# One weight array in order of use, two constant loads, tanh merge gates, new numbers in the order model, and two key tiles transposed back to back in a decoder block's attention

## The chip, the cores and the metric

The kernel runs on one core of a Trainium2 chip. The metric is the device time of one execution in microseconds (us). TensorE (PE in the profile) multiplies matrices and transposes, and a weight load (PEld) goes with each of its instructions. VectorE (DVE), ScalarE (ACT) and GpSimd (POOL) work element by element. SyncE (SP) issues the transfers (DMAs) in the kernel before.

## The reference, cut to what matters

```python
h = rms_norm(x, norm_pre); proj = h @ w_in            # x: 512 x 1024, w_in: 1024 x 6936, float32
q_n,k_c,v_c,k_s,v_s,k_w,v_w,g_n,z_n,q_r,k_r,v_r,z_r,m_a,m_b = split(proj)
# mixer A: sparse attention, 8 heads of 64 in 2 groups, causal: compressed, selected and window branch
o_a = g0 * attend(q_n, kc, vc) + g1 * attend(q_n, k_s, v_s) + g2 * attend(q_n, k_w, v_w)
#   kc, vc = gelu((16-strided blocks of 32 keys + position table) @ w1) @ w2
y_a = (o_a * silu(z_n)) @ w_nsa_o
# mixer B: retention, 4 heads, chunks of 128 rows, group norm
y_b = (retention(rot(q_r), rot(k_r), v_r) * silu(z_r)) @ w_ret_o
merged = sigmoid(m_a) * y_a + sigmoid(m_b) * y_b
y = x + rms_norm(merged @ w_out, norm_post)
```

## The kernel before

**Arithmetic.** To keep float32 precision, each operand of a product is split into a high part `hi` (rounded to the format `FR` that TensorE takes at full rate) and a low part `lo = x - hi`. Each product is three matmuls (`mm3`: hi·hi, hi·lo, lo·hi), 128 rows by 512 columns for most. For each half of a weight block ScalarE (seldom VectorE) makes `whi<-raw`, and VectorE or GpSimd makes `wlo<-raw,whi` (`split_lo`, with `sub_split`). `either` picks GpSimd where the order model says that it would be done sooner.

**Stages on TensorE, in order.** Block A (the first 512 columns: keys and values; eight steps `k`, all four row tiles in each), block C (280 columns: more keys and values, the branch gates), Q, the two hidden layers of the compressed keys (`hidden`), and then the blocks of `PLAN`: Z, MA, ZR, QK, VR and so on, last the output projection. The work of attention and of retention stands between these matmuls. Around block A stands the start: the input arrives transposed in eight tiles (`load_xT`), is scaled by `gp` and split (`hTh`, `hTl`); `WAKE` matmuls on an identity matrix run before it.

**Attention.** `att_head` makes a score tile (L840 is its masked minimum, then `exp` on ScalarE, a reciprocal and a scaling on VectorE). `att_block` transposes the probabilities of four heads for one key tile into one PSUM bank (four float32 transposes, L220), ScalarE and VectorE split them, and two matmuls add their product with the values to `po`. Two banks, the ring `PT`, serve all transposes.

**Transfers.** A load takes 1024 columns of weights (512 KB) into one of four `raw` buffers; `load_next` issues it once the load four before it is split. All are issued from SP's queue in program order. The loads cut their rows out of the weight arrays as these are given, in runs of 1 or 2 KB; some need two DMAs. `const_loads` issues ten small DMAs: rotary table, position tables (four), gate bias, `w2` (four). `positions` brings the position tables into their layout with two transposes on TensorE, in the middle of block A.

**What sets the order.** Nothing is scheduled on the chip: every engine takes its instructions in the order written. The class `Order` walks through coroutines, one for each piece of work, and issues the one that its own clock says is ready (`od.pe`, `od.op`, `od.dma` add costs and hold each engine's time). `LAG` and `PE_LAG` are the delays that it allows between an engine's result and its use. An operation that in truth comes later than the model says makes its user wait on the chip.

**Gates.** `tail_m` makes `sgs = sigmoid(m * rsrow)` on ScalarE; `tail_ya` and `tail_yb` multiply it with `y_a` and `y_b`. The other functions in use at that time are `exp` and `tanh`.

Of the kernel before, what the change touches and what calls it, by code (L numbers as in the profile page):

```python
# [18 lines left out]
P = 128  # L19
# [12 lines left out]
LAG, PE_LAG = 150.0, 110.0  # L32
# [4 lines left out]
WAKE = 10  # L37
# [3 lines left out]
class Order:  # L41
# [5 lines left out]
    def __init__(self):  # L47
        self.now = 0.0
        self.eng = {"act": 0.0, "dve": 0.0, "pool": 0.0, "dma": 0.0}
        self.ring = 500.0  # L50
        self.port = 0.0
        self.cos, self.n = [], 0
        self.flags = set()
# [15 lines left out]
    def op(self, e, cost, r=0.0, port=False):  # L69

        self.eng[e] = self.begin(e, r, port) + cost + ISSUE
        if port:
            self.port = self.eng[e]
        return self.eng[e]

    def dma(self, nbytes, r=0.0, n=1):
        for _ in range(n):
            self.ring = max(self.ring, r + LAG) + 475
            self.eng["dma"] = max(self.eng["dma"], self.ring + 625) + nbytes / n / 360.0
        return self.eng["dma"] + 910 - LAG  # L80
# [31 lines left out]
class Ring:  # L112
# [11 lines left out]

    def put(self, x, r=0.0):
        self.free.append((r, x))
# [3 lines left out]
def block_kernel(ctx: ExitStack, tc, x, xT, g_pre, w_in, b_gate, pe_k, w1_k, w2_k,  # L130
                 pe_v, w1_v, w2_v, w_nsa_o, w_ret_o, w_out, norm_post,
                 rope_n, rope_r, dmask, out):
# [82 lines left out]
    def mm(ps, a, b, start, stop, r=0.0, cost=None):  # L215
        T.matmul(ps, a, b, start=start, stop=stop)  # L216
        return od.pe(cost or max(0.4435 * size(b) + 1, 107 if a.shape[-1] > 64 else 54), r)

    def tr(ps, a, idn, r=0.0):
        T.transpose(ps, a, idn)  # L220
        return od.pe(56 if a.dtype == FR else 109, r)
# [5 lines left out]

    def either(n, r):

        return "dve" if od.begin("dve", r, True) + 1.04 * n <= od.begin("pool", r, True) + 2.36 * n else "pool"  # L230
# [59 lines left out]
    loads = []  # L290

    def add_block(w, c0, n, nk, perm=False, single=0):
        for c in range(nk // 2):
            def ld(raw, c=c):
                if c < single:
                    for k in range(2):
                        r0 = c * 256 + k * P
                        DMA.dma_start(raw[:, k * n:(k + 1) * n], w[r0:r0 + P, c0:c0 + n])
                    return
                DMA.dma_start(raw[:, :2 * n].rearrange("p (k n) -> p k n", k=2),  # L300
                              w[c * 256:(c + 1) * 256, c0:c0 + n].rearrange("(k p) n -> p k n", p=P))
            loads.append((ld, 2 * n, 2 if c < single else 1, perm))

    def add_w1(w1):
        w1v = w1.rearrange("(h l d) n -> h d l n", h=2, l=16)
        for c in range(4):
            def ld(raw, c=c):
                for hf in range(2):
                    DMA.dma_start(raw[hf * 64:(hf + 1) * 64].rearrange("p (l n) -> p l n", l=4),
                                  w1v[hf][:, 4 * c:4 * c + 4, :])  # L310
            loads.append((ld, 1024, 2, False))

    def add_qk(hp):
        for c in range(4):
            def ld(raw, c=c):
                rv = raw.rearrange("p (k n) -> p k n", k=2)
                for i, c0 in enumerate((C_QR, C_KR)):
                    DMA.dma_start(rv[:, :, i * 256:(i + 1) * 256],
                                  w_in[c * 256:(c + 1) * 256, c0 + hp * 256:c0 + hp * 256 + 256]
                                  .rearrange("(k p) n -> p k n", p=P))  # L320
            loads.append((ld, 1024, 2, False))

    def add_nsa_o(half):
        for c in range(2):
            def ld(raw, c=c):
                rv = raw.rearrange("p (k n) -> p k n", k=2)
                for g in range(2):
                    DMA.dma_start(rv[g * 64:(g + 1) * 64],
                                  w_nsa_o[g * 256 + c * 128:g * 256 + (c + 1) * 128, half * 512:(half + 1) * 512]
                                  .rearrange("(k p) n -> p k n", p=64))  # L330
            loads.append((ld, 1024, 2, False))

    add_block(w_in, C_A, 512, KD, single=1)
    add_block(w_in, C_C, 280, KD)
    add_block(w_in, C_Q, 512, KD)
    add_w1(w1_k)
    add_w1(w1_v)
    for name, i in PLAN:
        if name == "Z":
            add_block(w_in, C_Z, 512, KD, True)  # L340
        elif name == "QK":
            add_qk(i)
        elif name == "NO":
            add_nsa_o(i)
        elif name == "RO":
            add_block(w_ret_o, i * 512, 512, KD)
        else:
            add_block(w_in, {"ZR": C_ZR, "VR": C_VR, "MA": C_MA, "MB": C_MB}[name] + i * 512, 512, KD)
    for half in range(2):
        add_block(w_out, half * 512, 512, KD)  # L350
# [8 lines left out]

    def load_next():  # L360
        i = len(raws)
        if i < len(loads):
            raw = rp.tile([P, 1024], FT, name="raw", tag="raw", bufs=NR)
            loads[i][0](raw)
            raws.append((raw, od.dma(P * loads[i][1] * 4, parts[2 * (i - NR) + 1][2] if i >= NR else 0.0, loads[i][2])))
# [9 lines left out]
    def splitter():  # L375
        for i, (_, n, _, perm) in enumerate(loads):
            for k in range(2):
# [17 lines left out]
                if perm:  # L395
                    src = src.rearrange("p (g j c) -> p g j c", g=2, j=4)
                    vh, vl = (v.rearrange("p (j g c) -> p g j c", g=2, j=4) for v in (vh, vl))
# [70 lines left out]
    gp = cp.tile([P, KD], FT, name="gp")  # L468
    ss = cp.tile([P, NT], FT, name="ss")
# [55 lines left out]
    ropen = cp.tile([P, NT, 32], FT, name="ropen")  # L525
    bg = cp.tile([P, 24], FT, name="bg")
# [3 lines left out]
    pes = [cp.tile([P, 16], FT, name=f"pe{i}") for i in range(2)]  # L530
    pen = [at(40 + 0.5 * i, P)[0:32] for i in range(2)]
# [46 lines left out]
    def vals(src, br, t, r):  # L578
        for g in range(2):
            sv = src[:, g * 64:(g + 1) * 64]  # L580
            e = act(VS[:, t, br, g, g, :], sv, r=r)
            e = sub_split(VS[:, t, br, g, 1 - g, :], sv, VS[:, t, br, g, g, :], e, either(64, e))
        return e

    def tail_a(t, ps, e, ring):
# [13 lines left out]
        yield od.need("pos")  # L599
# [261 lines left out]
    def att_block(t, g, br, b, kt, slots, lastblk):  # L861
# [3 lines left out]
        pt = yield from PT.get()  # L865
        for j in range(4):
            e = tr(pt[:, j * P:(j + 1) * P], slots[j]["pv"][:, b, kt * P:(kt + 1) * P], ident, r)
        if lastblk:
            for s in slots:
                PR.put(s["P"], e)  # L870
        phl = yield from PHL.get()
# [31 lines left out]
    def att_unit(t, g, brs, slots):  # L903
        yield lambda: all("r" in s for s in slots)
        todo = [(br, b, kt) for b, br in enumerate(brs) for kt in range(t + 1)]
        for i, (br, b, kt) in enumerate(todo):
            od.spawn(att_block(t, g, br, b, kt, slots, i == len(todo) - 1), 2)
# [9 lines left out]
    def att_sum(t, g, po):  # L917
# [12 lines left out]
        e = tt(gv, low[m].rearrange("p (j c) -> p j c", j=4), gv, OP.mult, e, either(512, e))  # L930
# [37 lines left out]
    def tail_qk(hp, t, ps, e):  # L968
# [17 lines left out]
        on = either(512, e)  # L986
# [420 lines left out]
```

## Time and profile before

| what | us |
|---|---|
| three runs: median, lowest, highest | 536.37, 535.72, 537.97 |
| the profiled execution: its time | 536.74 |
| its span in the trace | 534.8 |
| busy in the span: TensorE, weight loads | 521.1, 437.2 |
| busy in the span: VectorE, ScalarE, GpSimd | 387.9, 265.2, 36.5 |

The span is the part of an execution that the trace shows. The profiled execution took 1.9 us more than its span, and stands 0.37 us above the median. Busy times of different engines overlap. A matmul of 512 columns is written as 0.39 us long, but the next one starts 0.227 us after it: the records overlap, and a short wait hides in them.

### The profile page before, as it was taken

How to read it: one execution, taken by the hardware profiler on the slowest of the kernel's cores; microseconds unless marked ns; L12 is line 12 of the kernel's file. 1: busy time of each engine (PE TensorE's matmuls, PEld its weight loads, DVE VectorE, ACT ScalarE, POOL GpSimd, SP SyncE). 2: the span in 40 equal slices, each digit the busy share in tenths (PEclk: the TensorE clock that was granted, in tenths of full speed). 3: DMA queues.
4: the chain of work that ended last, by engine and by line, in shares of the span. 5: the costliest groups of instructions: out<-in, count | busy, mean ns of one | idle time of the engine just before them, and what ended most of it. 6: DMA issues, size and time to landing. Idle time of an engine off the chain costs nothing.

```text
span 534.8 us, 7434 instructions
## 1 busy us (share of the span) xinstructions
PE 521.1 (97%) x2642; PEld 437.2 (82%) x2642; DVE 387.9 (73%) x911; ACT 265.2 (50%) x560; POOL 36.5 (7%) x50
## 2 busy tenths in 40 slices
PE   8989998999999999999999999999999999999995
PEld 7778787888788887888888888888888888888885
DVE  6589889889698889999867877796746245346433
ACT  6562588456689576375645243553414234114411
POOL 1000020000004000030000120100000000000000
PEclk9999999999999999999999999999999999999999
DMA  8861137514014013251321424130825052404022
GB/s 313 295 215 56 43 80 235 159 30 110 21 39 119 1 34 100 65 158 41 96 82 43 135 63 134 40 120 13 301 79 144 14 157 84 146 8 157 2 88 108
DMA packets 34837, 55.22 MB, mean 103 GB/s; under 512 B 4336, under 2 KB 14448, under 8 KB 34800
## 3 DMA queue, kind: packets, MB, share of 16 engines
q1 hardware_dynamic: 34800, 54.75, 33.3%
q8 instruction: 20, 0.33, 0.2%
q14 instruction: 17, 0.14, 0.1%
HBM read 52.64 MB, written 2.10 MB: 102 GB/s over the span
## 4 chain that ended last, share of the span: by engine, by line
PE 78%; DVE 10%; DMA 5%; ACT 3%; issue 2%; SPq 1%; POOL 0%; POOLq 0%; DVEq 0%; ACTq 0%
PE bank L216 73%; PE bank L220 5%; DVE arena_f L195 3%; DVE wlo L195 2%; DMA arena_f<-in_x_dram 2%; DVE arena_r L195 1%; DMA arena_f<-in_xT_dram 1%; DMA raw<-in_w_in_dram 1%; ACT arena_f L183 1%; ACT L183 1%; ACT arena_r L183 1%; DMA raw<-in_cmp_w_v_dram 1%; DVE arena_f L204 1%; DVE arena_f L208 1%; DVE arena_f L840 1%
## 5 line engine op out<-in xcount | busy, mean ns | idle before, releaser
L183 ACT ACTIVATE whi<-raw 128x512 fp32r<-128x512 f32 x150 | 90.2, 626 | 55.9 <-PE bank L216 47.3
L195 DVE TENSOR_TENSOR wlo<-raw,whi 128x512 fp32r<-128x512 f32 x145 | 96.3, 699 | 12.3 <-ACT whi L183 10.4
L216 PE MATMUL bank<-whi,hTh 128*128 128x512 f32 x256 | 99.6, 404 | 0.1
L216 PE MATMUL bank<-wlo,hTh 128*128 128x512 f32 x256 | 96.6, 392 | 0.1
L216 PE MATMUL bank<-whi,hTl 128*128 128x512 f32 x256 | 96.3, 391 | 0.0
L216 PE MATMUL bank<-arena_r 128*128 128x256 f32 (+2 forms) x328 | 70.3, 335 | 0.6 <-DVE stat L840 0.4
L183 ACT ACTIVATE arena_r<-bank 128x512 fp32r<-128x512 f32 (+2 forms) x80 | 44.6, 570 | 39.6 <-PE bank L220 35.6
L216 PE MATMUL bank<-hTh,whi 128*128 128x512 f32 x160 | 63.7, 398 | 0.0
L216 PE MATMUL bank<-hTh,wlo 128*128 128x512 f32 x160 | 62.5, 391 | 0.0
L216 PE MATMUL bank<-hTl,whi 128*128 128x512 f32 x160 | 62.4, 390 | 0.0
L216 PE MATMUL bank<-arena_r,whi 128*128 128x512 f32 x192 | 59.1, 389 | 0.0
L216 PEld LDWEIGHTS bank<-arena_r 128*128 128x128 f32 x328 | 51.3, 189 | 7.8 <-DVE stat L840 0.9
L216 PEld LDWEIGHTS bank<-whi,hTl 128*128 128x128 f32 x256 | 48.0, 188 | 10.6
L216 PEld LDWEIGHTS bank<-wlo,hTh 128*128 128x128 f32 x256 | 48.1, 188 | 8.8 <-DVE wlo L195 0.8
L216 PEld LDWEIGHTS bank<-whi,hTh 128*128 128x128 f32 x256 | 48.0, 188 | 8.4 <-ACT whi L183 0.3
L195 DVE TENSOR_TENSOR arena_r<-bank,arena_r 128x512 fp32r<-128x512 f32 (+2 forms) x72 | 46.6, 655 | 9.3 <-ACT arena_r L183 8.7
L216 PE MATMUL bank<-whi,arena_r 128*128 128x512 f32 (+1 forms) x176 | 48.8, 352 | 0.0
L220 PE MATMUL bank<-ident,arena_f 128*128 128x128 f32 (+2 forms) x262 | 39.4, 274 | 4.6 <-DVE arena_f L560 2.6
L220 PEld LDWEIGHTS bank<-ident,arena_f 128*128 128x128 f32 (+2 forms) x262 | 31.2, 139 | 13.6 <-DVE arena_f L560 3.3
L216 PEld LDWEIGHTS bank<-arena_r,whi 128*128 128x128 f32 x192 | 36.0, 188 | 7.5
L216 PE MATMUL bank<-arena_r,wlo 128*128 128x512 f32 x96 | 37.3, 389 | 0.0
L183 ACT ACTIVATE arena_f<-arena_f,stat 128x512 f32<-128x512 f32 (+3 forms) x64 | 35.3, 555 | 2.2 <-DVE stat L840 2.1
(124 smaller groups left out, 708.7 us busy)
## 6 DMA issues: line engine op xcount, KB each, us to landing
raw<-in_w_in_dram SPq DMA_DIRECT2D x43, 512.0 KB, 4.5
raw<-in_w_in_dram SPq DMA_DIRECT2D x18, 256.0 KB, 3.1
arena_f<-in_x_dram SPq DMA_DIRECT2D x8, 512.0 KB, 6.3
raw<-in_w_ret_o_dram SPq DMA_DIRECT2D x8, 512.0 KB, 4.8
raw<-in_w_out_dram SPq DMA_DIRECT2D x8, 512.0 KB, 4.3
arena_f<-in_xT_dram SPq DMA_DIRECT2D x8, 256.0 KB, 5.2
raw<-in_cmp_w_k_dram SPq DMA_DIRECT2D x8, 256.0 KB, 3.8
arena_f<-in_rope_r_dram SPq DMA_DIRECT2D x8, 256.0 KB, 2.7
```

What stands on the lines that cost most here:

```text
L183: S.activation(o, i, func, **kw)
L195: (V if e == "dve" else G).tensor_tensor(o, a, b, op=op)
L204: V.tensor_scalar(o, a, s1, s2, op0=op0, op1=op1)
L208: V.scalar_tensor_tensor(o, a, s, b, op0=op0, op1=op1)
L216: T.matmul(ps, a, b, start=start, stop=stop)
L220: T.transpose(ps, a, idn)
L840: V.tensor_tensor_reduce(pv[:, b, :], sv[:, b, :], maskp[:, 512 - L:512], 1.0, -NEG, OP.add, OP.min, nm[:, b:b + 1])
```

## The change

1. All weights lie in one array `stream` in the order of use, each load as 128 rows that are contiguous (4 KB a row); the rows' order for Z is made there too. A load is one DMA (the first one two, and of these the first is issued from ScalarE's queue by `queue`).
2. The constants come in two DMAs, `small` into the tile `cst` (rotary table, gate bias, position tables in their final layout) and `w2s`. `positions`, its two transposes and its four copies are gone.
3. `gp` is loaded from ScalarE's queue; the first weight load is issued ahead of the masks and of the identity matmuls, of which there are 8 in place of 10.
4. The merge gates are `tanh(m/2)`, with 1 added in the product (`stt`); the factor 2 goes into the constant of the last norm (4e-6 for 1e-6).
5. `either` is gone: VectorE does the 15 `wlo` and three smaller operations that GpSimd did.
6. The order model: `LAG`, `PE_LAG`, a `TAIL` for each engine, a price for each change of TensorE between float32 and `FR` operands, and at most eight DMAs in flight.
7. `att_blocks` takes both banks of `PT` and transposes two key tiles, eight transposes, back to back.

```diff
-LAG, PE_LAG = 150.0, 110.0
+LAG, PE_LAG = 55.0, 60.0
+TAIL = {"act": 110.0, "dve": 82.0, "pool": 45.0}
-WAKE = 10
+WAKE = 8
...
-    def pe(self, cost, r=0.0):
-        self.now = max(self.now, r + LAG + PE_LAG) + cost
-        return self.now + 75
+    def pe(self, cost, r=0.0, exact=False):
+        if exact != self.exact:
+            cost += 100.0 if exact else 85.0
+            self.exact = exact
+        self.now = max(self.now, r + LAG) + cost
+        return self.now + 170.0
...
-        return self.eng[e]
+        return self.eng[e] + TAIL[e]
...
+    def both(self):
+        while len(self.free) < 2:
+            yield lambda: len(self.free) >= 2
+        (r, x), (r2, y) = self.free.pop(0), self.free.pop(0)
+        yield max(r, r2) + self.lag
+        return x, y
...
+    def queue(i, j):
+        return S if i + j == 0 else DMA
...
-            loads[i][0](raw)
+            for j, n in enumerate(loads[i][1]):
+                queue(i, j).dma_start(raw[:, c:c + n], ws[o:o + P * n].rearrange("(p n) -> p n", p=P))
...
-        r = sub_split(vl, src, vh, r, either(size(vl), r))
+        r = sub_split(vl, src, vh, r)
...
-        yield od.need("pos")
...
-    def att_block(t, g, br, b, kt, slots, lastblk):
+    def att_blocks(t, g, todo, slots, lastblk):
...
-        pt = yield from PT.get()
-        for j in range(4):
-            e = tr(pt[:, j * P:(j + 1) * P], slots[j]["pv"][:, b, kt * P:(kt + 1) * P], ident, r)
+        pts = (yield from PT.both()) if len(todo) > 1 else ((yield from PT.get()),)
+        for (br, b, kt), pt in zip(todo, pts):
+            for j in range(4):
+                e = tr(pt[:, j * P:(j + 1) * P], slots[j]["pv"][:, b, kt * P:(kt + 1) * P], ident, r)
+            od.spawn(att_half(t, g, br, kt, pt, e), 2)
...
-        e = act(sgs[i], sgs[i], AF.Sigmoid, r=e)
+        e = act(sgs[i], sgs[i], AF.Tanh, r=e, scale=0.5)
...
-        e = tt(sgs[ft], sgs[ft], ps, OP.mult, e)
+        e = stt(sgs[ft], sgs[ft], 1.0, ps, OP.add, OP.mult, e)
...
-        for i, p_ in enumerate((pe_k, pe_v)):
-            for k in range(2):
-                DMA.dma_start(pen[i][:, k * 64:(k + 1) * 64], p_)
-        constr["pos"] = od.dma(P * 512, n=4)
...
+        DMA.dma_start(cst, small)
+        constr["rope"] = od.dma(P * 736)
+        DMA.dma_start(at(38, 512), w2s)
+        od.dma(P * 2048)
...
-    DMA.dma_start(gp, g_pre)
-    load_xT(0)
...
+    S.dma_start(gp, g_pre)
+    load_xT(0)
+    load_next()
```

**SP's queue during block A.** Before, ten constant DMAs (from `ropen` on; `arena_f` holds the position tables and `w2`) stand between the second and the third load of block C's weights (128x2x280):

```order
L300 DMA raw<-in_w_in_dram 128x2x280
L481 DMA arena_f<-in_x_dram 128x1024
L1227 DMA ropen<-in_rope_n_dram 128x4x32
L1231 DMA arena_f<-in_cmp_pe_k_dram 32x64 x2
L1231 DMA arena_f<-in_cmp_pe_v_dram 32x64 x2
L1233 DMA bg<-in_b_nsa_gate_dram 128x24
L1236 DMA arena_f<-in_cmp_w_k_dram 128x2x64 x2
L1236 DMA arena_f<-in_cmp_w_v_dram 128x2x64 x2
L300 DMA raw<-in_w_in_dram 128x2x280 x2
L300 DMA raw<-in_w_in_dram 128x2x512 x4
```

The same place in the changed kernel:

```order
L323 DMA raw<-in_stream_dram 128x560
L441 DMA arena_f<-in_x_dram 128x1024
L1190 DMA cst<-in_small_dram 128x184
L1192 DMA arena_f<-in_w_dram 128x512
L323 DMA raw<-in_stream_dram 128x560 x2
L323 DMA raw<-in_stream_dram 128x1024 x8
```

Two DMAs stand now where ten stood, and the loads of block C and Q follow them.

**TensorE at the start of block C.** The first transposes (L220, L234 in the changed kernel) take block A's keys from `arena_f`; the 280-column matmuls around them are block C. Before:

```order
L216 MATMUL bank_88<-wlo,hTh 128x512
L216 MATMUL bank_81<-arena_r,hTh 128x280 x2
...
L216 MATMUL bank_81<-arena_r,hTh 128x280 x2
L216 MATMUL bank_81<-arena_r,hTl 128x280
L220 MATMUL bank_85<-ident,arena_f 128x128 x2
L216 MATMUL bank_81<-arena_r,hTh 128x280 x2
```

After, with all rows from block A's last matmul on:

```order
L230 MATMUL bank_88<-wlo,hTh 128x512
L230 MATMUL bank_81<-arena_r,hTh 128x280 x2
L230 MATMUL bank_81<-arena_r,hTl 128x280
L230 MATMUL bank_81<-arena_r,hTh 128x280 x2
L230 MATMUL bank_81<-arena_r,hTl 128x280
L230 MATMUL bank_81<-arena_r,hTh 128x280 x2
L230 MATMUL bank_81<-arena_r,hTl 128x280
L230 MATMUL bank_81<-arena_r,hTh 128x280 x2
L230 MATMUL bank_81<-arena_r,hTl 128x280
L230 MATMUL bank_81<-arena_r,hTh 128x280 x2
L230 MATMUL bank_81<-arena_r,hTl 128x280
L234 MATMUL bank_85<-ident,arena_f 128x128 x2
```

Five groups of three matmuls stand ahead of the first transposes now, where six stood before.

**ScalarE where the first merge gates stand between the exponentials.** `sg` are the gates of the block MA; rows that write `stat` are `exp`. Before:

```order
L183 ACT_TABLE_LOAD
L183 ACTIVATE sg_104<-sg_104 128x512
L183 ACTIVATE arena_r<-bank_85 96x512
L183 ACTIVATE arena_r<-bank_86 128x512
L183 ACT_TABLE_LOAD
L183 ACTIVATE arena_f,stat<-arena_f,stat 128x512 x2
L183 ACT_TABLE_LOAD
L183 ACTIVATE sg_105<-sg_105 128x512
L183 ACT_TABLE_LOAD
L183 ACTIVATE arena_f,stat<-arena_f,stat 128x512
```

After:

```order
L197 ACTIVATE sg_104<-sg_104 128x512
L197 ACTIVATE arena_r<-bank_86 96x512
L197 ACTIVATE sg_105<-sg_105 128x512
L197 ACTIVATE arena_r<-bank_85 128x512
L197 ACTIVATE arena_r<-bank_86 128x512
L197 ACTIVATE arena_f,stat<-arena_f,stat 128x384 x2
```

The table loads around the gates are gone; in the whole program one is left of ten, at the start. On TensorE the number of places where float32 work follows `FR` work, or the other way, falls from 141 to 123 in the two programs.

## Rows read from the trace of the kernel before

**Rows 1.** By stage: busy of PE, PEld, DVE, ACT, POOL; clock; DMA share, GB/s.

```profile
28.60:62.00 33.40, 30.57 (x190) 26.25 (x189) 31.30 (x94) 16.74 (x41) 1.28 (x4) 1.00 0.32 99
62.00:97.00 35.00, 33.30 (x200) 28.09 (x199) 29.19 (x76) 28.80 (x64) 4.13 (x3) 1.00 0.53 152
...
176.00:240.00 64.00, 63.95 (x329) 52.83 (x328) 60.02 (x165) 40.23 (x104) 6.59 (x6) 1.00 0.26 72
```

**Rows 2.** Timeline of the start: SP's queue, ACT, PE.

```profile
0.73 0.38 SPq L1325 DMA_DIRECT2D gp<-in_norm_pre_dram  x1
1.17 0.42 SPq L476 DMA_DIRECT2D arena_f<-in_xT_dram  x1
...
4.00 0.72 ACT L183 ACTIVATE hTh<-arena_f,gp 128x512 fp32r<-128x512 f32 x1 [1.78 <-DMA arena_f<-in_xT_dram]
...
5.29 0.97 PE L216 MATMUL bank<-whi,hTh 128*128 128x512 f32 x3
```

**Rows 3.** Timeline of PE around the two position transposes.

```profile
20.14 1.07 PE L216 MATMUL bank<-whi,hTl 128*128 128x512 f32 x4
21.55 0.22 PE L220 MATMUL bank<-ident,arena_f 32*128 32x32 f32 x1 [0.34 <-DMA arena_f<-in_cmp_pe_k_dram]
...
24.03 0.40 PE L216 MATMUL bank<-whi,hTl 128*128 128x512 f32 x1
```

**Rows 4.** Timeline, 13 to 34: SP's queue, ACT, DVE, PE.

```profile
13.62 0.38 SPq L1227 DMA_DIRECT2D ropen<-in_rope_n_dram  x1
...
22.29 5.99 SPq L300 DMA_DIRECT2D raw<-in_w_in_dram  x6
...
29.41 0.64 ACT L183 ACTIVATE whi<-raw 128x512 fp32r<-128x512 f32 x1 [2.06 <-DMA raw<-in_w_in_dram]
...
29.95 1.25 ACT L183 ACTIVATE nat<-bank,rs 128x512 f32<-128x512 f32 x2
...
31.96 0.42 DVE L195 TENSOR_TENSOR arena_f<-nat,ropen 128x64 f32<-128x64 f32 x3
...
33.28 0.44 PE L220 MATMUL bank<-ident,arena_f 128*128 128x128 f32 x2 [2.23 <-DVE arena_f L560]
```

**Rows 5.** PEld's waits from 33.6 to 62: waited for, us, times, longest.

```profile
PEld bank L220 <- DVE arena_r L195: 0.9, 2, 0.6
...
PEld bank L220 <- DVE arena_f L195: 0.2, 1, 0.2
```

**Rows 6.** Timeline of ACT and PE, 142 to 149 and 168 to 175.

```profile
144.58 1.28 ACT L183 ACT_TABLE_LOAD   x1
145.88 0.72 ACT L183 ACTIVATE arena_f<-arena_f,stat 128x512 f32<-128x512 f32 x1
...
146.04 0.49 PE L220 MATMUL bank<-ident,arena_f 128*128 128x128 f32 x3
147.53 0.76 PE L220 MATMUL bank<-ident,arena_f 128*128 128x128 f32 x5 [1.00 <-DVE arena_f L204]
...
168.97 1.28 ACT L183 ACT_TABLE_LOAD   x1
...
172.81 0.62 PE L216 MATMUL bank<-arena_r 128*128 128x384 f32 x2 [0.37 <-DVE stat L840]
...
174.81 0.61 PE L216 MATMUL bank<-arena_r 128*128 128x384 f32 x2 [0.21 <-DVE arena_f L195]
```

**Rows 7.** Timeline of PE: eight transposes at 78.94, four at 203.62.

```profile
78.94 1.03 PE L220 MATMUL bank<-ident,arena_f 128*128 128x128 f32 x8
...
203.62 0.60 PE L220 MATMUL bank<-ident,arena_f 128*128 128x128 f32 x4
...
204.52 0.40 PE L216 MATMUL bank<-whi,hTl 128*128 128x512 f32 x1
```

**Rows 8.** GpSimd's `wlo` as a group; VectorE's timeline at 297.

```profile
L195 POOL TENSOR_TENSOR wlo<-raw,whi 128x512 fp32r<-128x512 f32 x15 | 20.8, 1395 | 180.7 <-ACT whi L183 119.6 <-DVE stat L840 31.6 <-PE bank L216 29.5
...
297.05 2.99 DVE L195 TENSOR_TENSOR wlo<-raw,whi 128x512 fp32r<-128x512 f32 x3
```

More of the change, by code (lines that the diff above doesn't have):

```diff
@@ L304, in add_w1 @@
[L304 to L333, printed above, removed]
@@ L349, in block_kernel @@
-    for half in range(2):
-        add_block(w_out, half * 512, 512, KD)
+    loads, off = [], 0
+    for pieces in stream_shape():
+        loads.append((off, pieces))
+        off += P * sum(pieces)
     raws, parts, done = [], [], []
@@ L375, in splitter @@
     def splitter():
-        for i, (_, n, _, perm) in enumerate(loads):
+        for i, (_, pieces) in enumerate(loads):
+            n = sum(pieces)
             for k in range(2):
@@ L529, in block_kernel @@
     vcs = cp.tile([96, 2, 2, 64], FR, name="vcs")
-    pes = [cp.tile([P, 16], FT, name=f"pe{i}") for i in range(2)]
-    pen = [at(40 + 0.5 * i, P)[0:32] for i in range(2)]
+    pes = [cst[:, NT * 32 + 24 + 16 * i:NT * 32 + 40 + 16 * i] for i in range(2)]
     w2 = [at(38 + i, 256).rearrange("p (k r c) -> p k r c", k=2, r=2) for i in range(2)]
@@ L905, in att_unit @@
         todo = [(br, b, kt) for b, br in enumerate(brs) for kt in range(t + 1)]
-        for i, (br, b, kt) in enumerate(todo):
-            od.spawn(att_block(t, g, br, b, kt, slots, i == len(todo) - 1), 2)
+        for i in range(0, len(todo), 2):
+            od.spawn(att_blocks(t, g, todo[i:i + 2], slots, i + 2 >= len(todo)), 2)
     def att_out():
@@ L1323, in main @@
                     od.spawn(tail_o(t, half + j, half * 512 + j * n, n, ps, e), 1)
-    DMA.dma_start(gp, g_pre)
-    load_xT(0)
-    S.activation(ss[:, 0:1], nhalf[:, 0:1], AF.Square)
-    masks()
-    for _ in range(WAKE):
-        T.matmul(banks[0][:, 0:P], ident, ident, start=True, stop=True)
     hook[0] = [lambda: load_xT(1), lambda: load_xT(2)]
@@ L1338, in block_kernel @@
     hook[5] = [lambda: load_x(3), const_loads]
-    for i in range(NR):
+    S.dma_start(gp, g_pre)
+    load_xT(0)
+    load_next()
+    S.activation(ss[:, 0:1], nhalf[:, 0:1], AF.Square)
+    masks()
+    for _ in range(WAKE):
+        T.matmul(banks[0][:, 0:P], ident, ident, start=True, stop=True)
+    for i in range(1, NR):
         load_next()
@@ L1375, in _tables, with stream_shape, stream, block @@
     return rope_n, rope_r.reshape(2, SEQ, 512), dmask
-_INS = ["w_in", "b_nsa_gate", "cmp_pe_k", "cmp_w1_k", "cmp_w2_k", "cmp_pe_v", "cmp_w1_v",
-        "cmp_w2_v", "w_nsa_o", "w_ret_o", "w_out", "norm_post"]
+def stream_shape():
+    yield [512, 512]
+    yield from [[1024]] * 3
+    yield from [[560]] * 4
+    yield from [[1024]] * (4 + 8)
+    for name, _ in PLAN:
+        yield from [[1024]] * (2 if name == "NO" else 4)
+    yield from [[1024]] * 8
+def stream(a):
+    w_in, w_out = np.asarray(a["w_in"]), np.asarray(a["w_out"])
+    cols = lambda c0, n=512: w_in[:, c0:c0 + n]
+    pair = lambda w: list(w.reshape(-1, 2, P, w.shape[1]).transpose(0, 2, 1, 3).reshape(-1, P, 2 * w.shape[1]))
+    def block(name, i):
+        if name == "Z":
+            return pair(cols(C_Z).reshape(D, 2, 4, 64).transpose(0, 2, 1, 3).reshape(D, 512))
+        if name == "QK":
+            return pair(np.concatenate([cols(C_QR + i * 256, 256), cols(C_KR + i * 256, 256)], axis=1))
+        if name == "NO":
+            w = np.asarray(a["w_nsa_o"])[:, i * 512:(i + 1) * 512].reshape(2, 4, 64, 512)
+            return pair(w.transpose(1, 0, 2, 3).reshape(512, 512))
+        if name == "RO":
+            return pair(np.asarray(a["w_ret_o"])[:, i * 512:(i + 1) * 512])
+        return pair(cols({"ZR": C_ZR, "VR": C_VR, "MA": C_MA, "MB": C_MB}[name] + i * 512))
+    first = pair(cols(C_A))
+    out = [first[0][:, 0:512], first[0][:, 512:1024]] + first[1:] + pair(cols(C_C, 280)) + pair(cols(C_Q))
+    for n in ("k", "v"):
+        w1 = np.asarray(a[f"cmp_w1_{n}"]).reshape(2, 4, 4, 64, 256)
+        out += list(w1.transpose(1, 0, 3, 2, 4).reshape(4, P, 1024))
+    for name, i in PLAN:
+        out += block(name, i)
+    for half in range(2):
+        out += pair(w_out[:, half * 512:(half + 1) * 512])
+    return np.concatenate([o.reshape(-1) for o in out])
 def kernel(**inputs):
```

111 lines of the change are left out of this document (35 added, 76 removed).

## The prediction

> **What bounds the kernel now.** I read the table of busy times by stage first. From 176 to 240 TensorE is busy for 63.95 of 64 us [rows 1], and behind that it is no emptier. Most of the program is therefore a sum of TensorE's own work, and the change leaves that sum as it is: it drops two small transposes and two identity matmuls out of 2626 instructions. What can be won lies where TensorE waits. In the same table it idles 2.8 us from 28.6 to 62 and 1.7 us from 62 to 97 [rows 1]. Then I went to the timeline at each place where TensorE starts late, and looked for what its releaser itself had waited for. A matmul's record is 0.39 us long and the next one starts 0.227 us after it (four of them end 1.07 us after the first start [rows 3]; less one length, that is three steps), so an idle time in a row is about 0.16 us shorter than the time lost. The reader should see five such places, with three different causes: SP's queue, the table loads, and VectorE's own load.
>
> **The change part by part.**
>
> *The start.* SP issues `gp` at 0.73 and the first tile of x behind it at 1.17; the first `hTh` starts when that tile lands, at 4.00, and the first real matmul at 5.29 [rows 2]. With `gp` and the first weight piece on ScalarE's queue the tile is issued where `gp` was: 1.17 - 0.73 = 0.44 us earlier. The gain is between nothing (the landing is set by something else) and 0.44; I take 0.4. ScalarE now issues two DMAs ahead of its first table load, some 0.8 us by SP's two rows, and it idled 1.78 us ahead of `hTh` [rows 2], which hides that. Two identity matmuls less cost nothing as long as they end before the first weights are split. **-0.4.**
>
> *Constants.* The two position transposes stand amid plain matmuls. From 20.14 to 24.03 TensorE starts three groups of four, twelve steps, 2.72 us; it took 3.89 [rows 3]. The difference goes with the transposes: **-1.2.**
>
> *SP's queue.* Ten constant DMAs are issued one by one from 13.62 on, and the next weights only from 22.29 [rows 4], 8.7 us later. The weights of Q land late, so `whi` starts at 29.41 after a wait of 2.06 us for a DMA. ScalarE takes its work in order, and the eviction of block A (`nat`) stands behind that `whi`, at 29.95; VectorE then starts the rotation at 31.96, and TensorE's first transposes start at 33.28 after 2.23 us idle [rows 4]. Two constant DMAs take the place of ten, so I expect the weights some 7 us earlier (8.7 x 8/10). Then `nat` can start where block A ends. The chain from the eviction to the transposes is 33.28 - 29.95 = 3.3 us in the trace, of which `wlo` and `whi` for the late weights take the part up to 31.96; without them it is 0.6 us of eviction and the 1.3 us from 31.96 on, 1.9 us. The changed order has five groups of three 280-column matmuls ahead of the transposes, about 15 x 0.127 = 1.9 us (280 columns at 0.227 us for 512, an estimate). That just meets. The loss was 2.23 + 0.16; I leave 0.1 of it: **-2.3**, with nothing as the other end.
>
> *What was late behind that.* VectorE is busy 31.30 of 33.40 us from 28.6 to 62 [rows 1] and started this stage late. The loads of TensorE's weights wait there in five rows of 0.9 to 0.2 us, 2.7 us in all [rows 5]. Most wait for results of the same chains. An earlier start of VectorE should take some: between nothing and 2.7, and I take **-1.0**, since VectorE's amount of work there stays.
>
> *Table loads.* A gate between two exponentials brings two table loads of 1.28 us. The one at 144.58 delays an `exp` to 145.88, and the transposes that need it wait: TensorE starts the next one at 147.53 after 1.00 us idle [rows 6]. The one at 168.97 delays the exponentials ahead of 172.81 and 174.81, where TensorE idles 0.37 and 0.21 [rows 6]. With `tanh` the changed order holds no load behind the first. The three stalls with the 0.16 that each record hides are 2.1 us; one is traced straight to a load and two through VectorE, which waits for the exponentials, so between 1.1 and 2.1: **-1.9.**
>
> By its rows a table load is 1.28 us, and the next instruction starts 0.02 us behind it [rows 6]. The Trainium skill, ScalarE: Activation LUTs, section What ACT_TABLE_LOAD costs, adds a drain of about 1.38 us to it, 2.66 us for every switch. By that the two places could give back up to 5.3 us (an estimate from that page) in place of 1.9; these rows show no such drain, and the measurement decides.
>
> *Pairs of transposes.* Eight transposes end 1.03 us after the first start, four 0.60: four more cost 0.43, 0.108 each. From the start of the four at 203.62 to the last matmul of the next group at 204.52 it is 0.90; two matmuls and four transposes are 0.45 + 0.43 = 0.88 [rows 7]. A change of format and back costs some 0.02, not the 0.185 of the new model. Nine pairs fewer (141 to 123 changes) give 0.2, at most 9 x 0.185 = 1.7: **-0.2.** The price may still spoil the order a little; that stands under the new waits.
>
> *GpSimd's work on VectorE.* Fifteen `wlo` and three smaller operations are, at a step of 0.61 us, at most 18 x 0.61 = 11 us more for VectorE. Against it, VectorE's own operations stretch beside GpSimd's: three `wlo` in a row took 2.99 us at 297 where a step of 0.61 makes 1.9 [rows 8], 1.1 us lost to one GpSimd `wlo` of 1.395 mean. Fifteen times that would be 16 us. So VectorE's net lies between +11 and -5. Where TensorE is full (176 to 240) VectorE has 4 us to spare and is covered by other matmuls [rows 1], and I take **0**; from 62 to 97, where it is busy 29.19 of 35, three operations of GpSimd come to it [rows 1] (+1.8 at most), and there I expect no gain at all.
>
> The Trainium skill, SBUF — State Buffer, section SBUF: two separate sides, has the shared pair of ports as an exclusive lock: a VectorE operation with two inputs in SBUF waits for all of a GpSimd operation that reads SBUF. By that page alone the 15 `wlo` could have held VectorE for all of their 20.8 us (an estimate), and the move would be a gain for it of up to 10 us; the rows at 297 show 1.1 of 1.4 us held, in a place where VectorE had such operations to do, and that is the less of the two.
>
> *New waits.* The model now lets TensorE use VectorE's result 82 + 55 + 60 = 197 ns after its modelled end where 260 was allowed before, and a ScalarE result after 225. Every group of transposes stands closer to its data, by up to 0.06 us, over some 60 groups (123 changes of format, two a group): nothing to 4 us. Since the stages behind 176 show next to no idle time under the old margins, I take the lower part: **+1.0.**
>
> The sum is -0.4 - 1.2 - 2.3 - 1.0 - 1.9 - 0.2 + 1.0 = -6.0. It is made against the profiled execution, 536.74 (534.8 of span and 1.9 around it, which stays): 530.7. The median of the runs shown is 0.4 below that execution, so a median of 530.3 to 530.7; I say **530.7**.
>
> **The rivals.**
>
> *The stall at 33.28 stays.* If VectorE's work, not SP's queue, sets it, the 2.3 and the 1.0 behind it are not won: 536.74 - 2.7 = 534.0. For it speaks how full VectorE is there; against it the DMA as releaser of `whi` and the order `whi`, `nat` on ScalarE. Chance 0.1.
>
> *The closer order waits.* All gains come, and the new waits cost 4 in place of 1: 533.7. For it: all margins shrink at once, and a price of 0.185 is charged where 0.02 is seen. Against it: a traced wait ends 0.05 us behind the record that released it (VectorE's copy ahead of 33.28), well inside 197 ns. Chance 0.13.
>
> *More is won.* No new waits, the rest of the 2.7 in [rows 5], and a part of the 1.7 from 62 to 97: -6.0 - 1.0 - 1.7 = 528.0. Chance 0.13.
>
> *VectorE becomes the bound (the other side).* Attention and retention bring it up to 11 us of work. If nothing comes back from GpSimd's absence and all of it shows as lateness of transposes, it is 536.74 - 7.0 + 11.0 = 540.7; slower than before it is from the point where 7 of the 11 are exposed. For it: 60.02 of 64 busy from 176 to 240. Against it: TensorE idles 0.05 there, so VectorE's work was covered by other matmuls, and the row at 297. Chance 0.05.
>
> **How the numbers follow.** The forecast holds 0.59, from 529 to 532.8. The measurement can tell about 0.5% from no change, 2.7 us: faster means below 533.7. Faster: 0.59 + 0.13 (more), half of the 0.13 and a little of the 0.1, 0.8. Same: 0.14. Slower: 0.06, with what I have not thought of. The range that leaves out 2 in 10: down to the middle of the rival with more, 528.2, up past the two that end at 533.7 and 534.0: 534.2.
>
> **What would show it.** The first real matmul near 4.9; no transposes in block A; the issue of weights without a gap from 13 to 22; `nat` directly behind block A and the first 128x128 transposes waiting under 0.3; one table load; no GpSimd `wlo`, and the `wlo` of VectorE near 0.7 without long ones; TensorE's idle time from 28.6 to 62 under 1.5 us. I would be wrong if waits of 0.1 to 0.5 us for VectorE turn up in many groups between 60 and 240, or if the weights still land late at 25 to 29.

## The result and the profile after

The changed kernel takes 531.49 us (median of 5 runs, 531.36 to 533.15) where the kernel before took 535.86 in the same series: a ratio of 0.9915, 95% interval 0.9892 to 0.9938. The profiled executions differ by 5.4 us: 531.36 with a span of 529.4, against 536.74 with 534.8.

Busy time by stage after, in the columns of [rows 1]. The second and the third window are those of [rows 1] moved by 4 us; the first one begins behind the first 128x128 transposes, where that of [rows 1] still has the stall ahead of them in it:

```profile
31.00:58.00 27.00, 25.21 (x154) 21.10 (x153) 25.44 (x78) 12.21 (x34) 0.94 (x4) 1.00 0.19 61
58.00:93.00 35.00, 34.67 (x209) 29.39 (x209) 31.38 (x83) 28.21 (x61) 0.00 (x0) 1.00 0.40 127
172.00:236.00 64.00, 64.00 (x332) 53.57 (x332) 60.14 (x176) 39.24 (x105) 0.00 (x0) 1.00 0.22 74
```

VectorE is as full as before or fuller; GpSimd has four small operations in the first window and none in the others. TensorE idles 1.8 us from 31 to 58; from 58 to 93 it is 0.3, where it was 1.7 in the stage from 62 to 97 [rows 1]. From 28 us to its last instruction TensorE idles 2.1 us, where it idled 6.2 before.

The waits of weight loads in the first of these stages:

```profile
PEld bank L234 <- DVE arena_f L519: 1.5, 2, 0.9
PEld bank L234 <- DVE arena_r L209: 1.2, 3, 0.8
PEld bank L234 <- DVE arena_f L209: 0.7, 1, 0.7
PEld bank L234 <- issue: 0.5, 1, 0.5
```

They add up to 3.9 us, where the rows of the stage before, taken behind its stall, gave 2.7 [rows 5]. By these waits the stage has become worse.

The timeline after, at the places of [rows 2], [rows 3], [rows 4] and [rows 6], and at some others that the experiments come back to:

```profile
0.72 0.40 ACTq L1274 DMA_DIRECT2D gp<-in_norm_pre_dram  x1
0.73 0.38 SPq L436 DMA_DIRECT2D arena_f<-in_xT_dram  x1
1.16 0.46 ACTq L323 DMA_DIRECT2D raw<-in_stream_dram  x1
1.17 0.42 SPq L323 DMA_DIRECT2D raw<-in_stream_dram  x1
...
3.71 0.72 ACT L197 ACTIVATE hTh<-arena_f,gp 128x512 fp32r<-128x512 f32 x1 [0.57 <-DMA gp<-in_norm_pre_dram]
...
5.10 0.63 ACT L197 ACTIVATE whi<-raw 128x512 fp32r<-128x512 f32 x1 [0.67 <-DMA raw<-in_stream_dram]
...
5.78 1.19 PE L230 MATMUL bank<-whi,hTh 128*128 128x512 f32 x4 [0.78 <-ACT whi L197]
...
7.74 1.08 PE L230 MATMUL bank<-wlo,hTh 128*128 128x512 f32 x4
...
21.35 1.07 PE L230 MATMUL bank<-wlo,hTh 128*128 128x512 f32 x4
22.25 1.07 PE L230 MATMUL bank<-whi,hTh 128*128 128x512 f32 x4
...
24.48 0.64 ACT L197 ACTIVATE whi<-raw 128x512 fp32r<-128x512 f32 x1 [1.04 <-DMA raw<-in_stream_dram]
...
27.27 1.27 ACT L197 ACTIVATE nat<-bank,rs 128x512 f32<-128x512 f32 x2 [0.35 <-PE bank L230]
27.99 0.43 DVE L209 TENSOR_TENSOR arena_f<-nat,cst 128x64 f32<-128x64 f32 x3 [0.25 <-ACT nat L197]
...
29.61 0.38 PE L234 MATMUL bank<-ident,arena_f 128*128 128x128 f32 x2
...
91.71 1.89 DVE L209 TENSOR_TENSOR wlo<-raw,whi 128x512 fp32r<-128x512 f32 x3
...
142.59 0.63 ACT L197 ACTIVATE sg<-sg 128x512 f32<-128x512 f32 x1 [2.69 <-DVE sg L209]
...
144.08 0.62 ACT L197 ACTIVATE arena_f<-arena_f,stat 128x384 f32<-128x384 f32 x1
...
161.75 0.60 PE L234 MATMUL bank<-ident,arena_f 128*128 128x128 f32 x4
...
250.68 1.03 PE L234 MATMUL bank<-ident,arena_f 128*128 128x128 f32 x8
...
256.40 0.67 ACT L197 ACTIVATE arena_r<-bank,rs 128x512 fp32r<-128x512 f32 x1
...
264.58 1.60 PE L230 MATMUL bank<-arena_r 128*128 128x256 f32 x12
```

`hTh` starts at 3.71, 0.29 earlier than in [rows 2], and waits for `gp`. The first real matmul comes at 5.78, later than the 5.29 of [rows 2]: the first `whi` waits for its weight piece until 5.10. In block A the groups of four now follow each other every 0.91 us with nothing between. Q's first `whi` stands at 24.48 in place of 29.41 [rows 4], `nat` follows block A directly, and the first 128x128 transposes start at 29.61 without a wait. Behind the gate `sg` at 142.59 no table load stands. Three `wlo` in a row take 1.89 us at 91.71, where [rows 8] had 2.99 beside GpSimd; eight transposes take 1.03 as in [rows 7].

### The profile page after: what moved, and what is told of

Same layout as the page of the kernel before. It is cut to its first block, busy times and chain, and to the rows that moved or that the text cites. A ratio compares the mean times of both kernels' runs of the same rounds, so it can differ in the third digit from the quotient of the medians.

```text
span 529.4 us, 7318 instructions
## 1 busy us (share of the span) xinstructions
PE 519.1 (98%) x2636; PEld 437.3 (83%) x2636; DVE 390.4 (74%) x925; ACT 253.4 (48%) x551; POOL 12.6 (2%) x32
## 4 chain that ended last, share of the span: by engine, by line
PE 89%; DVE 7%; issue 2%; DMA 1%; ACT 0%; POOLq 0%; DVEq 0%; POOL 0%; ACTq 0%
PE bank L230 83%; PE bank L234 6%; DVE arena_f L209 2%; DVE wlo L209 2%; DVE arena_r L209 1%; DMA raw<-in_stream_dram 1%; DVE arena_f L519 1%; DVE nat L209 0%; DVE arena_f L218 0%; DVE arena_f L798 0%; ACT nat L197 0%; DVE arena_f L222 0%; ACT whi L197 0%; POOLq L1389 0%; POOL rr L209 0%
## 5 line engine op out<-in xcount | busy, mean ns | idle before, releaser
L209 DVE TENSOR_TENSOR wlo<-raw,whi 128x512 fp32r<-128x512 f32 x160 | 103.2, 686 | 7.2 <-ACT whi L197 6.5
L234 PE MATMUL bank<-ident,arena_f 128*128 128x128 f32 (+1 forms) x260 | 37.1, 274 | 1.6 <-DVE arena_f L519 1.0
L234 PEld LDWEIGHTS bank<-ident,arena_f 128*128 128x128 f32 (+1 forms) x260 | 30.4, 138 | 8.4 <-DVE arena_f L519 1.5
```

What stands on the lines that cost most here:

```text
L209: (V if e == "dve" else G).tensor_tensor(o, a, b, op=op)
```

## The experiments

All runs are compared with the kernel before in their own series (medians 536.2 to 536.7). Over all series that kernel's median moved from 535.86 to 536.66, so a difference between medians of two series is uncertain by some 0.8 us.

| run | median, us | ratio to before, 95% |
|---|---|---|
| sigmoid_gates | 532.94 | 0.9928 to 0.9964 |
| ten_constants | 535.11 | 0.9967 to 0.9994 |
| start_on_sp | 531.80 | 0.9899 to 0.9933 |
| start_in_turn | 531.56 | 0.9905 to 0.9930 |
| old_order_model | 542.11 | 1.0086 to 1.0125 |
| old_model_pairs_apart | 540.80 | 1.0052 to 1.0088 |
| old_model_till_62 | 542.29 | 1.0085 to 1.0122 |
| order_edits_undone | 533.63 | 0.9939 to 0.9970 |
| order_edits_alone | 541.06 | 1.0078 to 1.0106 |
| pairs_apart | 531.49 | 0.9893 to 0.9930 |
| gpsimd_back | 537.16 | 0.9996 to 1.0019 |
| gpsimd_beside | 536.07 | 0.9996 to 1.0019 |

### The gates alone: sigmoid_gates

```diff
-        e = act(sgs[i], sgs[i], AF.Tanh, r=e, scale=0.5)
+        e = act(sgs[i], sgs[i], AF.Sigmoid, r=e)
```

The two products and the constant of the norm go back with it.

> The changed kernel with only the gates set back: sigmoid, a plain product, and 1e-6 in the last norm. Every instruction stands where it stood, so only table loads can come in. My term (a load of 1.28 us delays exponentials that transposes wait for, at two places): +1.9, by the two traces up to +2.3, so 533.4 to 533.8 where the changed kernel took 531.5, with TensorE's first transposes behind each of the two gate groups waiting 0.3 to 1.0 us. If each switch cost 2.66 us on the path, up to +5.3: 536.8. If the gain came from other things (the exponentials have slack in the new order): within 0.4 of 531.5.

It cost 1.45 us (532.94 for 531.49). ScalarE's group of table loads behind the start, busy and mean ns of one:

```profile
L197 ACT ACT_TABLE_LOAD x7 | 9.0, 1283 | 0.1
```

The timeline at the one place where TensorE waits for more than before:

```profile
158.04 1.28 ACT L197 ACT_TABLE_LOAD   x1
...
159.33 0.62 ACT L197 ACTIVATE arena_f<-arena_f,stat 128x384 f32<-128x384 f32 x1
...
163.09 0.66 PE L234 MATMUL bank<-ident,arena_f 128*128 128x128 f32 x4 [1.05 <-DVE arena_r L209]
```

The exponential starts 0.01 us behind its load, and the transposes wait 1.05 where the changed kernel has them at 161.75 without a wait. At 144.35 a load is back too and makes no transposes wait in the new order (the next ones start at 146.85). So the term holds for one of its two places. The Trainium skill, ScalarE: Activation LUTs, section What ACT_TABLE_LOAD costs, has a drain of 1.38 us on top of each load; the trace does not agree: the exponential starts 0.01 us behind the load, and the seven loads together cost the kernel 1.45 us.

### SP's queue: ten_constants

```diff
-        DMA.dma_start(cst, small)
+        for i in range(8):
+            DMA.dma_start(cst[:, 23 * i:23 * i + 23], small[:, 23 * i:23 * i + 23])
```

`w2s` is cut in two in the same way.

> The changed kernel with its two constant loads cut into ten DMAs at the same place of SP's queue; every other instruction stands where it stood. If the term of the prediction stands by itself, Q's weights land late again, TensorE idles some 2.4 us ahead of the first 128x128 transposes near 30, and the time rises by 2.3 to 533.8. If VectorE's amount of work sets the end of the stage behind it, the 2.4 us come back there but the waits of weight loads from 31 to 58 (3.9 us in the changed kernel, 2.7 in the old one from 33.6 to 62) fall by 1 to 1.5, and the time rises by about 1: 532.5. If the number of constant DMAs was not what made the weights late, 531.5.

It cost 3.6 us. The old chain is back, row for row as in [rows 4]:

```profile
12.88 7.41 SPq L1191 DMA_DIRECT2D cst<-in_small_dram  x8
...
21.75 10.14 SPq L323 DMA_DIRECT2D raw<-in_stream_dram  x8
...
28.26 0.64 ACT L197 ACTIVATE whi<-raw 128x512 fp32r<-128x512 f32 x1 [1.71 <-DMA raw<-in_stream_dram]
...
30.63 1.25 ACT L197 ACTIVATE nat<-bank,rs 128x512 f32<-128x512 f32 x2
...
32.78 0.69 PE L234 MATMUL bank<-ident,arena_f 128*128 128x128 f32 x2 [2.99 <-DVE arena_f L519]
```

By stage, columns as in [rows 1], directly behind the stall:

```profile
33.00:38.00 5.00, 5.00 (x31) 4.99 (x31) 4.44 (x24) 4.32 (x13) 0.24 (x1) 0.71 0.49 167
```

Ten DMAs where two stood are the cause: eight of them take SP 7.4 us, and the weights behind them are late. The waits of weight loads from 31 to 58 are 6.5 us here, 3.3 without the stall itself, 0.6 less than in the changed kernel. TensorE's granted clock is 0.71 from 33 to 38, behind 3 us in which it did nothing. TensorE's order is the same in both kernels, so their traces can be compared instruction by instruction: this run is 3.2 us late at the stall (32.78 for 29.61), 4.6 us late at 37.7, behind the low clock, and 3.9 us late from 43 on. So 0.7 us are paid back, less than the lower clock took. The rival that VectorE's work sets the end of this stage expected 1.0 to 1.5 us back and a time of 532.5; at 535.11 it falls.

### The start: start_on_sp and start_in_turn

start_on_sp has both edits, start_in_turn only the second.

```diff
-    S.dma_start(gp, g_pre)
+    DMA.dma_start(gp, g_pre)
...
-        return S if i + j == 0 else DMA
+        return DMA
```

> The changed kernel with gp and the first weight piece back on SP's queue, in the old order (gp, x tile, piece 1, piece 2). If the first piece came late because it shared the transfer engines with the second piece, which another queue had issued at the same moment (or because ScalarE's queue is slow to begin), it lands before the second one again, and the first real matmul starts at 5.3 or earlier in place of 5.78: about -0.5, 531.0. If something else of the start made it late (how its rows lie in the one array), the first matmul stays near 5.8 and the time at 531.5.

> The changed kernel with only gp on ScalarE's queue; both pieces of the first weight load follow the x tile on SP's queue. If the first piece came late because the second one, issued at the same moment on another queue, shared the transfer engines with it, the first piece lands near 4.4, its whi starts directly behind hTh at 4.4 and the first real matmul at 5.1 in place of 5.78: -0.6, 530.9. If gp on ScalarE's queue is what is late, hTh starts at 3.7 or later as before and the matmul at 5.1 to 5.3. If the layout of the one array delays the piece (it landed at 4.87 on SP's queue behind gp and the tile, where the old kernel had it before 4.63), the matmul stays at 5.5 or later.

The first real matmul started at 5.55 and at 4.91, and the time stayed the same (531.80, 531.56). The timeline of start_in_turn:

```profile
3.61 0.72 ACT L197 ACTIVATE hTh<-arena_f,gp 128x512 fp32r<-128x512 f32 x1 [0.94 <-DMA gp<-in_norm_pre_dram]
...
4.91 1.50 PE L230 MATMUL bank<-whi,hTh 128*128 128x512 f32 x4
...
7.29 1.21 PE L230 MATMUL bank<-wlo,hTh 128*128 128x512 f32 x4
...
24.00 1.45 ACT L197 ACTIVATE arena_r<-raw 128x280 fp32r<-128x280 f32 x4 [1.39 <-DMA raw<-in_stream_dram]
...
30.42 0.44 PE L234 MATMUL bank<-ident,arena_f 128*128 128x128 f32 x2 [0.94 <-DVE arena_f L519]
```

That the two pieces delay each other when two queues issue them together is shown: in turn, the first one is there when `hTh` is done, and its `whi` starts at 4.24 in place of 5.10. A slow queue of ScalarE is not the cause: in the changed kernel the piece on SP's queue, issued at 1.17, lands at 4.88, hardly earlier than the 5.08 of the other; in turn the pieces land at 4.17 and 5.45. But it wins nothing. Of the 0.87 us half are lost at the third group (7.29 for 7.74), and all and more at 30.42, where TensorE waits 0.94. The weights of block C (128x280) land at 24.00, in the changed kernel at 21.93. From 5 to 20 the transfers of both kernels are full by the row of busy time (DMA share 1.01 and 1.03), so I take it that this stretch hangs on their end and not on the first matmul; no run moves that end by itself.

### The order model, GpSimd and the pairs

pairs_apart and gpsimd_back each take one edit back. old_order_model takes `Order` and its numbers back; old_model_pairs_apart takes the pairs back too, order_edits_undone GpSimd's share as well (the diff shows the core of the last two). order_edits_alone is the kernel before with these three edits only.

```diff
-LAG, PE_LAG = 55.0, 60.0
+LAG, PE_LAG = 150.0, 110.0
...
-        r = sub_split(vl, src, vh, r)
+        r = sub_split(vl, src, vh, r, either(size(vl), r))
```

> The changed kernel with the order model as it was before (150 and 110 ns, no price for a change of format, no limit of DMAs in flight). All of the order on TensorE and VectorE is planned anew. If the closer margins made the waits from 31 to 58, these fall from 3.9 to 2.7 us or less and the time by 1 or more: 530.5. If VectorE's amount of work makes them, they stay near 4 and the time within 0.5 of 531.5. If the new numbers are worth something behind 58 (waits there fell from 2.9 to 1.4 up to 93, and from 1.3 to 0.7 behind 172), it is 1 to 2 us more: 532.5 to 533.5.

> The changed kernel with the transposes of attention one key tile at a time, as before; new order model, no GpSimd (139 changes of format on TensorE in place of 123). By my term (0.02 us for each pair of changes): +0.2, 531.7. If a pair of changes costs the 0.185 us of the new model on the chip: 8 x 0.185 = 1.5, 533.0. If the pairs only help or harm by the order that they bring about, anything within 2 us either way, and the waits would then sit in a few single places.

> The changed kernel with the choice between VectorE and GpSimd as before; new order model, pairs kept. The planner now gives GpSimd 12 wlo and 5 smaller operations. By my term: 0, 531.5 within 0.5. If GpSimd's operations hold VectorE for all of their time, VectorE loses up to 12 x 1.4 = 17 us and gains 12 x 0.65 = 8 us, and if a third of the net shows on TensorE it is +3: 534.5. If VectorE's amount of work makes the waits from 31 to 58 and those behind 172, it is 1 to 2 us less: 530.

> Only the edits that don't concern the order: one weight array, two constant loads, tanh, the new start; with the order model as before, GpSimd's share and single transposes. If these edits carry the whole gain (3.6 us by the run with ten constants, 1.4 by the run with sigmoid, 1.2 for the position transposes, less 0.5 at the start: 5.7 less than 536.2), 530.5, and the old order model was bad only together with one of the other two. If the old model is bad with any other edit, near 540. If the new order model itself is worth something, between: 532 to 535.

> The changed kernel with the old order model and single transposes, without GpSimd. With the pairs the old model took 542.1. If the pairs were what it could not place (both banks have to be free at once), 531 to 533. If it was GpSimd's share on VectorE, for which the old model's due times are wrong, it stays above 538, with waits for VectorE in few large pieces between 200 and 275.

> The kernel before with only the order model's new numbers, the pairs of transposes, and without GpSimd's share. If the order edits are worth the same with and without the others (2.1 us less than with the other edits alone): 534.1. If their gain needs weights that are on time: 536 or more. If they win in the places that the others left behind as well (more cover from 62 to 97): 533 or less.

The pairs are worth nothing (531.49 with and without). The other two can't be priced one by one. Medians, all with the other edits of the change in (single transposes in the first row, pairs in the second):

| | GpSimd has a share | VectorE alone |
|---|---|---|
| old numbers | 533.63 | 540.80 |
| new numbers | 537.16 | 531.49 |

Without GpSimd the kernel loses 7.2 us under the old numbers and wins 5.7 under the new ones. Not all of the 7.2 us need be the order's: the profiled executions of all three orders with old numbers and VectorE alone lose some 2 us at the start, in instructions that stand in the same order everywhere (last section). How many of their other executions do is not shown; those of old_model_pairs_apart run from 538.92 to 541.87. And the order edits alone cost 4.8 us in the kernel before (541.06 against 536.3).

Waits of weight loads by stage show where this sits (sums of the rows of each trace, us):

| kernel | 31 to 58 | 58 to 93 | 236 to 316 |
|---|---|---|---|
| changed | 3.9 | 1.4 | 0.3 |
| order_edits_undone | 2.5 | 4.0 | 2.1 |
| old_model_pairs_apart | 2.5 | 2.9 | 7.0 |
| old_order_model | 2.5 | 2.8 | 7.3 |
| gpsimd_back | 3.8 | 1.2 | 3.0 |

The new numbers do make the waits from 31 to 58, with and without GpSimd, and they take as much or more away from 58 to 93. The largest differences stand in the last column. For gpsimd_back it explains 2.7 of the 5.7 us.

### One place in the order: old_model_till_62

It uses the old numbers until the order model's clock passes 56 us, and the new ones from there on.

```diff
+            if self.old and self.now > SWITCH:
+                self.old, LAG, PE_LAG = False, 55.0, 60.0
```

> The changed kernel with the old order model's numbers for the stretch up to about 60 us (on TensorE the order is that of the run with the old model for the first 313 matmuls and transposes), and the new numbers behind it. If the new numbers make the waits from 31 to 58 (all runs with the new model wait there some 1.7 us longer than those with the old one), these waits fall to 2.5 us, and if the rest is planned as well as before, the time falls by 1.5: 530.0. If the order of the later stages hangs on how the stage before it ended, the gain may be lost in single waits of 0.5 to 1.2 us behind 60: 531.5 or more.

The waits from 31 to 58 fell to 2.5, and the time rose to 542.29, far outside what was expected. Its timeline at 262, and behind it TensorE's clock from 266.4 to 273.2 in the columns of [rows 1]:

```profile
261.96 1.03 PE L251 MATMUL bank<-ident,arena_f 128*128 128x128 f32 x8
...
265.30 0.59 ACT L214 ACTIVATE nat<-bank 64x512 f32<-64x512 f32 x1 [1.55 <-PE bank L247]
...
267.27 0.69 DVE L226 TENSOR_TENSOR arena_f<-nat,arena_f 64x512 f32<-64x512 f32 x1
...
268.44 1.41 DVE L239 SCALAR_TENSOR_TENSOR arena_r<-bank,rs,arena_r 128x512 fp32r<-128x512 f32 x2
...
269.25 0.80 PE L247 MATMUL bank<-whi,hTh 128*128 128x512 f32 x1 [3.58 <-DVE arena_r L239]
```

```profile
266.40:273.20 6.80, 3.95 (x9) 3.14 (x10) 4.51 (x9) 1.77 (x4) 0.00 (x0) 0.50 0.35 119
```

At 261.96 stand attention's last transposes. In `ret` the eviction of a values block (`arena_r<-bank,rs`, which frees the accumulator bank) has to wait for the flags `att20` to `att31`, because it writes where attention's queries lay. Here both banks are full before attention is done, and TensorE idles 3.58 us. The stall costs more than that: the granted clock is 0.50 until 273.2, the lower of its two levels (1.2 GHz), and the nine matmuls from 269.25 to 273.23 take 4.0 us, where nine steps of 0.227 make 2.0. The weight load that waits here 3.7 us waits 3.1 in old_order_model and in old_model_pairs_apart, and there the granted clock is 0.54 and 0.52 from 266 to 273. In the changed kernel the last transposes come at 250.68, an eviction of the values block at 256.40 and retention's matmuls at 264.58; the matmuls in between cover attention's end, and TensorE is busy for all 80 us from 236 to 316. Numbers that differ by some 0.1 us thus decide, 200 us later, whether there is a stall of 3 to 4 us and 2 us of low clock behind it. In the profiled executions this run is 11.2 us behind the changed kernel (542.52 for 531.36); the stall and the clock are 5.7 of them, other waits of weight loads from 236 to 316 some 2.5, the slower start about 2.

### GpSimd's operations by themselves: gpsimd_beside

```diff
+        if p in BESIDE:
+            G.tensor_tensor(spare, src[:, :496], f(vh)[:, :496], op=OP.subtract)
         r = sub_split(vl, src, vh, r)
```

> The changed kernel with its order untouched on TensorE, VectorE and ScalarE, and 12 additional GpSimd subtractions of 128x496, whose result nothing uses, beside the 12 wlo that GpSimd took in the run with its share back (they read the same raw and whi). If a GpSimd operation holds VectorE's operations with operands in SBUF, VectorE's instructions beside them stretch by 1 to 1.8 us, TensorE waits for them, and the time rises by 1.5 to 4: 533 to 535.5, although VectorE has the same work as in the changed kernel. If the 4 to 5.7 us of that run came from the new order alone, and not from GpSimd's operations, the time stays at 531.5 within 0.5.

It cost 4.6 us, with the order of the other engines unchanged. The timeline at the first 128x128 transposes, at the first added operation, and at the place of the changed kernel's row 91.71:

```profile
30.20 0.44 PE L235 MATMUL bank<-ident,arena_f 128*128 128x128 f32 x2
...
41.74 1.25 POOL L367 TENSOR_TENSOR spare<-raw,whi 128x496 f32<-128x496 f32 x1
...
91.19 5.07 POOL L367 TENSOR_TENSOR spare<-raw,whi 128x496 f32<-128x496 f32 x3 [42.32 <-ACT whi L198]
...
94.12 3.29 DVE L210 TENSOR_TENSOR wlo<-raw,whi 128x512 fp32r<-128x512 f32 x3
...
98.07 0.44 PE L235 MATMUL bank<-ident,arena_f 128*128 128x128 f32 x2 [0.70 <-DVE arena_r L210]
```

The busy row of the page, first of the changed kernel and then of this one, each by itself:

```profile
PE 519.1 (98%) x2636; PEld 437.3 (83%) x2636; DVE 390.4 (74%) x925; ACT 253.4 (48%) x551; POOL 12.6 (2%) x32
```

```profile
PE 521.1 (98%) x2636; PEld 437.1 (82%) x2636; DVE 396.4 (74%) x925; ACT 253.5 (47%) x551; POOL 29.6 (6%) x44
```

The same three `wlo` take 3.29 us in place of 1.89, and TensorE waits for what stands behind them. Over the kernel VectorE's same 925 instructions take 6.0 us longer beside 17.0 us more of GpSimd, nearly all of it in eight instructions that ran beside an added one. Not all of the 4.6 us is GpSimd's, though: TensorE's first real matmul is at 6.16 (5.78 in the changed kernel) and its first transposes are at 30.20 (29.61), 0.6 us late ahead of the first added operation at 41.74. Some 4 us are left. The Trainium skill, SBUF — State Buffer, section SBUF: two separate sides, has the shared ports as an exclusive lock. The trace agrees that VectorE is held; by the page alone it could have been all 17.0 us (an estimate), measured are 6.0.

## Why the prediction came out, step by step

The time (531.5 for 530.7) came out, but as a sum in which wrong steps offset each other; that it came so close is in part luck.

- **The start (-0.4): wrong.** The first matmul came 0.49 later, not 0.4 earlier, since the first piece shared the transfers with the second, and `hTh` won 0.29 of 0.44, held by `gp`. Moreover the step has no price here: three starts from 4.91 to 5.78 gave the same time.
- **Constants (-1.2): right by the trace**, the groups of four follow without a gap. No run undid this alone.
- **SP's queue (-2.3): right**, the stall is gone, and ten DMAs brought it back. They cost 3.6 and not 2.3, with a lower clock behind the stall that the kernel before does not show (1.00 from 28.6 to 62 [rows 1]). A slip without effect: 280 columns at 0.227 for 512 are 0.124, not 0.127; fifteen of them are 1.9 either way.
- **What was late behind it (-1.0): wrong.** With the old numbers these waits stay at 2.5 (2.7 before), with the new ones they grow to 3.9.
- **Table loads (-1.9): the mechanism is right, the size is that of one place**: 1.45 in the changed order.
- **Pairs (-0.2): nothing**, within what can be told.
- **GpSimd's work (0): wrong.** I set the stretching of VectorE against its added work and let them cancel; in the new order GpSimd's operations alone cost some 4 of the 4.6 measured.
- **New waits (+1.0): right from 31 to 58** (+1.2 from 2.7 to 3.9), but the new order wins as much from 58 to 93 (2.9 to 1.4), which I had not counted.

I had priced the edits that don't concern the order at -6.8 and the rest at +0.8. Measured, the first alone give -2.9 (536.55 to 533.63), and the second a further -2.1 on top (533.63 to 531.49). The error in the method is the sum itself: each edit makes the order anew, and what it wins at its own place can come back as a wait elsewhere. The rival with VectorE as the bound, 540.7, is about what three orders without GpSimd gave (540.8 to 542.3). But its condition was another one: not VectorE's amount of work, which is 390.4 us in the changed kernel too, but the place of attention's end, with the lower clock behind it and the slower start.

What stays open: which of the new numbers moves attention's end, how the 5.7 us of gpsimd_back divide between GpSimd's operations and the order, and why the order edits alone cost 4.8 us in the kernel before; there the waits from 33.6 to 62 are 4.8 us (2.7 before) and from 145 to 176, where the table loads stand, 3.9 (2.3). None of the runs beats the changed kernel beyond what can be told.

## What to carry to other kernels

Where a planner writes the order, try a change of its numbers and a change of an engine's share in all four combinations: here, from the old numbers with GpSimd's share, each of the two alone loses 3.5 to 7 us, and both together win 2. Price GpSimd's help by what it does to VectorE's operations beside it, not by the work that it takes over. And before buying an earlier first matmul, look whether the transfers of the first stage are full. Behind a stall, read the granted clock: here stalls of 3.0 and 3.6 us cost another 1.4 and 2.0.

## What the runs showed of the hardware

In some profiled executions the first real matmuls ran at half their pace. The timeline of TensorE in old_order_model, where they follow the identity matmuls after an idle time as in the changed kernel:

```profile
5.66 2.08 PE L222 MATMUL bank<-whi,hTh 128*128 128x512 f32 x4 [0.53 <-ACT whi L189]
7.54 1.91 PE L222 MATMUL bank<-whi,hTl 128*128 128x512 f32 x4
9.24 1.06 PE L222 MATMUL bank<-wlo,hTh 128*128 128x512 f32 x2
```

The second and the third group start 1.70 us apart, 0.43 for each matmul of 512 columns; in the changed kernel's profile the groups stand 0.91 apart. Behind the stall in old_model_till_62 the same step of 0.43 goes with a granted clock of 0.50, but here the row of granted clock says 1.00 for 5 to 10 in both runs. All three orders with the old numbers and VectorE alone have nine or ten such steps, about 2 us each. order_edits_undone, which has the old numbers too, has none. TensorE's first 377 instructions stand in the same order there as in old_order_model, and yet its first 128x128 transposes start at 29.86 and those of old_order_model at 32.16; the 2.3 us are not made up. So this part of the time comes from no order. What decides it is not shown.
